# A decoder trunk on one core: two gate tiles moved from the attention to the front of the seven-product units, and the branches' elementwise work drawn together

## The chip, the cores and the metric

The kernel runs as one program on one core of a Trainium2 chip. Its time is the device time of one execution in microseconds; of several runs the median is taken. The engines are PE (TensorE, matrix products), DVE (VectorE, elementwise), ACT (ScalarE, activations and copies), POOL (GpSimd) and SP (SyncE, which here only starts transfers). Each engine works through its own queue in order and meets the others through semaphores.

## The reference, cut to what matters

Two layers over a sequence of 1024 tokens with 1024 channels, in float32. Each layer:

```python
h = rmsnorm(x, norm_mix_g[l])
q, k, v, f_logit, cx, cb, cc, px, gate_logit = split(h @ w_in[l])
a = forgetting_attention(rmsnorm(q), rmsnorm(k), v, log_sigmoid(f_logit + forget_b[l]))  # 8 heads of 64
y_attn = a @ w_attn_out[l]
y_conv = (cb * conv3(cc * cx)) @ w_conv_out[l]                # depthwise, 256 channels
y_pool = pooling_mixer(px, pool_w[l], pool_scale[l])          # trailing means over 2, 4, 8, 16 positions
g = sigmoid(gate_logit)                                       # three gates of 1024 channels
x = x + (g[0] * y_attn + g[1] * y_conv + g[2] * y_pool) @ w_o[l]
h = rmsnorm(x, norm_ffn_g[l])
x = x + (silu(h @ w_gate) * (h @ w_up)) @ w_ffn_out[l]
```

## The kernel before, in words

Everything is kept transposed: 128 channels on the partitions, the tokens in two halves of 512 along the free axis. Every float32 operand is split into a high and a low part that TensorE multiplies at full rate, and each product is three matmuls: high by high, high by low, low by high (mm3, lines 219 to 221). The split of a weight tile is one cast on ACT (L115) and one subtraction on DVE (L116); of an activation tile, a cast (L224) and a subtraction (L225). Raw weights (tag "wr") have two slots, the high and low parts (tags "wh" and "wl") three; the weight pieces of the seven-product units use the same three.

A layer goes through these stages:

1. v and the forget logits (v_run; v_evac writes v to DRAM through staging tiles whose four tags vtags turn).
2. Eleven seven-product units (sevens, m_unit). Each makes a block of 256 output channels by 1024 tokens with seven products in place of eight. The products are over sums and differences of parts of h, the forms: b11, b21 and b22 are parts of h, t1 to t4 are made by make_form on DVE and ACT, four tiles each, every tile with a high and a low part. prepare makes the units' weight pieces, four to a unit. The eleven units compute q, k, the conv and pool branches' inputs (which go to DRAM) and six gate tiles (SGATES).
3. The attention, four pairs of heads, eight query blocks and two heads a pair. scores, turn and values are issued one chain apart, and between them fill issues steps of gate tiles. A gate tile (gate_unit) is a projection of 128 gate channels: for each half of the tokens 24 matmuls, in four steps, then a Tanh from PSUM on ACT (L667) and a store to DRAM (gate_away, on SP). GATES says how many of them there are: two before the first pair and three in each pair.
4. The last four gate tiles. Between their steps the branches' elementwise work is issued: for each half c of the branch channels the loads cc_in and fetch, then cx_evac, cb_evac and px_evac, nearly all on DVE.
5. The merge (merge_unit): output projections of the three branches, gated and added. The gate tiles are fetched from DRAM by get_t; those in the set plain were stored as raw logits and get their Tanh there (L1082).
6. The output projection, norms and the feed-forward part.

The helper `plan` is a queue of units; `step` runs the next step of the current unit, and `prefetch` loads weights for the units ahead as long as no more than two tiles are pending. The framework places the instructions of each engine in a queue of its own making, by the order of the program and by what its timing model takes to be ready; the order within a stage can therefore differ from that of the text.

The tiles of stage 2 that matter here come from one ring of five buffers, which the forms t1 and t3 and the copies of the products share:

```python
def mring(name, dt=F32):
    return mp.tile([P, HN], dt, tag="ring", name=name, bufs=MRING)   # MRING = 5
```

In make_form the four tiles of t1 stay in the ring (diffs); t2 is made from them in place, and t4 from t2. In a unit the first product is copied out of its bank into the ring (copy("p1"), L837), and the fourth product is then accumulated on the same bank.

Of the kernel before, what the change touches and what calls it, by code (L numbers as in the profile page):

```python
# [9 lines left out]
F32 = mybir.dt.float32  # L10
F32R = mybir.dt.float32r
# [5 lines left out]
P = 128  # L17
S = 1024
D = 1024
KT = D // P  # L20
NH = 2
HN = S // NH
# [6 lines left out]
OFF_CX, OFF_CB, OFF_CC, OFF_PX, OFF_G = 1544, 1800, 2056, 2312, 2568  # L29
# [12 lines left out]
FINE = 4  # L42
# [1 line left out]
TURNS_LAST = {3: ((1, 2),), 4: ((3, 2),), 6: ((5, 2),), 7: ((6, 1), (7, 1))}  # L44
QDEF = 2
SGATES = 6
GATES = (2, 3, 3, 3, 3)


class Unit:  # L50
# [9 lines left out]
def trunk_kernel(ctx: ExitStack, tc: tile.TileContext, x, norm_mix_g, w_in, forget_b, q_norm_g, k_norm_g,  # L60
# [37 lines left out]
    plan = deque()  # L98
# [49 lines left out]
    def prefetch():  # L148

        pending = sum(len(u.specs) for u in plan if u in loaded_w)  # L150
        for u in plan:
            if u in loaded_w:
                continue
            if pending and pending + len(u.specs) > LOOK:
                break
            loaded_w[u] = [load_f(s) if s[1] == "f" else load(s) for s in u.specs]
            pending += len(u.specs)
# [36 lines left out]
    def drain():  # L194
        while step():
            pass
        while later:
            run_later(True)

    def wspec(src, rows, c0, cols):  # L200

        return (src[rows[0]:rows[1], c0:c0 + cols].rearrange("(k p) m -> p k m", p=P), ((rows[1] - rows[0]) // P, cols))
# [342 lines left out]
    for l in range(L):  # L545
# [7 lines left out]
        def mring(name, dt=F32):  # L553
            return mp.tile([P, HN], dt, tag="ring", name=name, bufs=MRING)
        win = w_in[l]
# [26 lines left out]

        v_dram = [dr.tile([P, 2, KT, P], F32R, tag=f"vd{p}", name="vd") for p in range(PAIRS)]

        vtags = deque(("q2", "q3", "qkh", "qkl"))

        def v_evac(p0, n, banks):

            for q in range(2):
                for j in range(0, 4, 2):  # L590
                    tag = vtags[0]
                    vtags.rotate(-1)
                    dst = mp.tile([P, HN], F32R, tag=tag, name="vst").rearrange("p (e j c) -> p e j c", e=2, j=2)
                    for jj in range(2):
                        src = banks[j + jj][:, q * P:(q + 1) * P].rearrange("p (e c) -> p e c", e=2)
                        A.copy(out=dst[:, :, jj, 0:HD], in_=src)
                        V.tensor_tensor(out=dst[:, :, jj, HD:P], in0=src, in1=dst[:, :, jj, 0:HD].bitcast(F32),
                                        op=ALU.subtract)
                    G.dma_start(out=v_dram[p0 + q][:, :, 4 * n + j:4 * n + j + 2, :], in_=dst)
# [58 lines left out]
        def gate_away(br, m, n, t):  # L658
            td = dr.tile([P, HN], F32, tag=f"td{br}{m}{n}", name="td")
            nc.sync.dma_start(out=td, in_=t)  # L660
            spilled.add((br, m, n))
            tgate[br, m, n] = td
# [133 lines left out]
        def make_form(name):  # L796

            add_h = lambda k, n, part: h[k, n][part].bitcast(F32)
            for k in range(KH):
                if name in ("t1", "t3"):  # L800
                    x, y = ((k, 1), (k, 0)) if name == "t1" else ((KH + k, 1), (k, 1))
                    t = mring("form")
                    lows = mp.tile([P, HN], F32, tag="q1", name="lows")
                    V.tensor_tensor(out=t, in0=add_h(*x, 0), in1=add_h(*y, 0), op=ALU.subtract)
                    V.tensor_tensor(out=lows, in0=add_h(*x, 1), in1=add_h(*y, 1), op=ALU.subtract)
                    V.tensor_tensor(out=t, in0=t, in1=lows, op=ALU.add)
                else:
                    x = (KH + k, 1) if name == "t2" else (KH + k, 0)
                    t = diffs[k]
                    V.tensor_tensor(out=t, in0=add_h(*x, 0), in1=t, op=ALU.subtract)  # L810
                    V.tensor_tensor(out=t, in0=t, in1=add_h(*x, 1), op=ALU.add)
                if name == "t1":
                    diffs[k] = t
                hi = mp.tile([P, HN], F32R, tag=f"{name}h{k}", name=name)
                lo = mp.tile([P, HN], F32R, tag=f"{name}l{k}", name=name)
                hilo(hi, lo, t)
                mforms[name].append((hi, lo))

        def m_unit(u):
            kind, at = pairs[u]  # L820
            t = {}

            def finish(e, n, src):
                if kind == "g":
                    br, m = divmod(at + e, KT)
                    gate_away(br, m, n, src)
                    plain.add((br, m, n))
                elif kind in ("cc", "cx", "cb", "px"):
                    branch[kind, e, n] = dr.tile([P, HN], F32, tag=f"{kind}{e}{n}", name="brd")
                    nc.sync.dma_start(out=branch[kind, e, n], in_=src)  # L830
                else:
                    norm_qk(at + e, kind, n, src)

            def copy(name):
                def ev(bank):
                    t[name] = mring(name)
                    return A.copy(out=t[name], in_=bank)  # L837
                return ev

            def add(name, e, n):  # L840
                def ev(bank):
                    done = V.tensor_tensor(out=t[name], in0=bank, in1=t[name], op=ALU.add)
                    finish(e, n, t[name])
                    return done
                return ev

            def c21(bank):
                t["c21"] = mring("c21")
                A.copy(out=t["c21"], in_=bank)
                finish(1, 0, t["c21"])  # L850

            def u2(bank):
                done = copy("u2")(bank)
                if u == 0:
                    make_form("t4")
                return done

            seven(u, mforms, {"p1": copy("p1"), "c11": add("p1", 0, 0), "p5": copy("p5"), "u2": u2,
                              "c12": add("u2", 0, 1), "c22": add("p5", 1, 1), "c21": c21})

        next_first.run = v_run(0)
# [2 lines left out]
        for _ in range(FINE * NH):  # L864
            step()
        plan.append(Unit([wspec(win, (r, r + D // 2), OFF_V + 2 * P, 2 * P) for r in (0, D // 2)], v_run(2)))
        prefetch()
        prepare(0)
        make_form("t1")
        for _ in range(FINE):  # L870
            step()
        make_form("t2")
        drain()
        prepare(1)
        make_form("t3")
        for _ in range(SGATES):
            gates.popleft()
        for u in range(len(work)):
# [252 lines left out]
        for c in range(2):  # L1131
            cc_in(c)
            for n in range(NH):
                cx_evac(c)(n, fetch("cx", c, n))
                for _ in range(FINE):
                    step()
            for n in range(NH):
                cb_evac(c)(n, fetch("cb", c, n))
                px_evac(c)(n, branch["px", c, n])
                for _ in range(FINE):  # L1140
                    step()
        for mm in range(4):
            plan.append(merge_unit(mm))
        prefetch()
# [290 lines left out]
        u = n_in  # L1435
# [73 lines left out]
```

## Time and profile before

| what | value |
|---|---|
| median of 3 runs | 2873.04 us (2869.07 to 2873.19) |
| the profiled execution | 2866.68 us |
| its span, first to last instruction | 2864.9 us |
| mean granted clock of TensorE | 0.992 of full speed |

The profile is of one execution. Times within it count from the first instruction. Layer 0 takes about the first half of the span: v to about 78 us, the units to about 310, the attention to about 580, the last gates to about 621, then the merge. Layer 1 has the same stages some 1422 us later.

### The profile page before, as it was taken

The page shows a single profiled execution, that of the slowest core. Times are in us where ns is not written, and L with a number is a line of the kernel's source. Part 1 is how long each engine was busy: PE and PEld are TensorE (multiplying, and loading weights), DVE is VectorE, ACT ScalarE, POOL GpSimd, SP SyncE. Part 2 cuts the span into 40 slices and gives each one's busy share as a digit, 9 for nine tenths or more (in the row PEclk, how much of TensorE's full clock was granted, in tenths as well). Part 3 has the DMA queues.
Part 4 walks back from the last instruction along what each step waited for, and adds up shares of the span by engine and source line. Part 5 has one row for each costly group of instructions (what it writes and reads, how often), then busy time and mean ns, then how long its engine had stood idle before and what let it go on. Part 6 is the DMA issues. An engine that isn't in the chain of part 4 may idle for free.

```text
span 2864.9 us, 38079 instructions
## 1 busy us (share of the span) xinstructions
PE 2807.6 (98%) x13224; PEld 2322.3 (81%) x13224; DVE 2080.1 (73%) x3869; ACT 1313.2 (46%) x2137; POOL 584.7 (20%) x1100
## 2 busy tenths in 40 slices
PE   8899999999999999999998999999999999999999
PEld 8788888878888888878796888888788888888887
DVE  8886298878575676758788763988785867766675
ACT  5665266533453444432356643655334444444222
POOL 2110333000411111334010104330003111223430
PEclk9999999999999999999999999999999999999999
DMA  7343856267533444699353438552765244557992
GB/s 226 114 129 111 213 140 159 78 221 226 187 104 118 133 143 152 204 289 310 111 150 105 140 100 224 140 157 84 249 214 181 95 133 147 162 162 232 309 284 93
DMA packets 378089, 481.90 MB, mean 168 GB/s; under 512 B 35336, under 2 KB 227336, under 8 KB 376872
## 3 DMA queue, kind: packets, MB, share of 16 engines
q1 hardware_dynamic: 261864, 260.19, 29.4%
q0 software_dynamic: 116032, 219.27, 25.9%
q8 instruction: 104, 1.70, 0.2%
q14 instruction: 89, 0.73, 0.1%
HBM read 319.91 MB, written 159.45 MB: 167 GB/s over the span
## 4 chain that ended last, share of the span: by engine, by line
PE 84%; DVE 6%; DMA 5%; issue 3%; ACT 1%; POOL 0%; SPq 0%; DVEq 0%; ACTq 0%; POOLq 0%
PE dps L219 25%; PE dps L221 25%; PE dps L220 25%; PE pt L738 2%; PE pv L755 2%; DMA td<-tg 1%; PE qk L713 1%; PE qk L714 1%; DMA px<-brd 1%; DVE wl L116 1%; PE dps L615 1%; PE dps L617 1%; PE dps L616 1%; DMA acd<-al 1%; DMA wr<-in_w_in_dram 1%
## 5 line engine op out<-in xcount | busy, mean ns | idle before, releaser
L219 PE MATMUL dps<-t,wsh 128*128 128x512 f32 x992 | 388.5, 392 | 17.5 <-ACT p L837 17.5
L220 PE MATMUL dps<-t,wsh 128*128 128x512 f32 x992 | 387.6, 391 | 0.0
L221 PE MATMUL dps<-t,wsl 128*128 128x512 f32 x992 | 387.4, 391 | 0.0
L221 PE MATMUL dps<-hh,wsl 128*128 128x512 f32 x744 | 289.8, 390 | 0.0
L219 PE MATMUL dps<-hh,wsh 128*128 128x512 f32 x744 | 289.7, 389 | 0.0
L220 PE MATMUL dps<-hl,wsh 128*128 128x512 f32 x744 | 289.6, 389 | 0.0
L378 ACT CAST wsh<-ws 128x1024 fp32r<-128x1024 f32 (+2 forms) x172 | 167.3, 973 | 253.6 <-DVE ws L370 176.7
L219 PE MATMUL dps<-hh,wh 128*128 128x512 f32 x704 | 278.7, 396 | 0.0
L220 PE MATMUL dps<-hl,wh 128*128 128x512 f32 x704 | 278.0, 395 | 0.0
L221 PE MATMUL dps<-hh,wl 128*128 128x512 f32 x704 | 277.1, 394 | 0.0
L379 DVE TENSOR_TENSOR wsl<-wr,wsh 128x512 fp32r<-128x512 f32 (+4 forms) x172 | 151.1, 878 | 158.0 <-ACT wsh L378 157.8
L379 DVE TENSOR_TENSOR wsl<-ws,wsh 128x1024 fp32r<-128x1024 f32 (+2 forms) x172 | 193.0, 1123 | 87.7 <-ACT wsh L378 87.7
L219 PEld LDWEIGHTS dps<-t,wsh 128*128 128x128 f32 x992 | 187.1, 189 | 57.8 <-ACT p L837 18.4
L115 ACT CAST wh<-wr 128x1024 fp32r<-128x1024 f32 (+1 forms) x116 | 118.4, 1021 | 231.6 <-PE dps L220 171.6
L116 DVE TENSOR_TENSOR wl<-wr,wh 128x1024 fp32r<-128x1024 f32 (+1 forms) x116 | 138.1, 1191 | 112.8 <-ACT wh L115 112.6
L221 PEld LDWEIGHTS dps<-t,wsl 128*128 128x128 f32 x992 | 187.2, 189 | 39.2
L220 PEld LDWEIGHTS dps<-t,wsh 128*128 128x128 f32 x992 | 187.2, 189 | 38.5
L378 ACT CAST wsh<-wr 128x512 fp32r<-128x512 f32 (+4 forms) x172 | 133.6, 777 | 134.5 <-PE dps L220 132.2
L1196 POOL DMA_DIRECT2D acd<-ah x122 | 64.9, 532 | 547.0 <-ACT ah L224 544.2
L221 PE MATMUL dps<-ach,wsl 128*128 128x512 f32 x448 | 174.6, 390 | 0.0
L219 PE MATMUL dps<-ach,wsh 128*128 128x512 f32 x448 | 174.4, 389 | 0.0
L220 PE MATMUL dps<-acl,wsh 128*128 128x512 f32 x448 | 174.4, 389 | 0.0
(271 smaller groups left out, 6550.7 us busy)
## 6 DMA issues: line engine op xcount, KB each, us to landing
wr<-in_w_ffn_in_dram SPq DMA_DIRECT2D x40, 1024.0 KB, 5.5
acl<-acd POOLq DMA_DIRECT2D x136, 256.0 KB, 6.8
ach<-acd POOLq DMA_DIRECT2D x136, 256.0 KB, 6.6
acd<-ah POOLq DMA_DIRECT2D x122, 256.0 KB, 2.3
acd<-al POOLq DMA_DIRECT2D x122, 256.0 KB, 2.5
tin<-td SPq DMA_DIRECT2D x96, 256.0 KB, 3.7
wr<-in_w_in_dram SPq DMA_DIRECT2D x44, 512.0 KB, 4.1
wr<-in_w_in_dram SPq DMA_DIRECT2D x22, 1024.0 KB, 5.3
```

The costliest lines, as they stand in the source:

```text
L115: A.copy(out=hi[:, 0:cnt], in_=rv)
L116: V.tensor_tensor(out=lo[:, 0:cnt], in0=rv, in1=hi[:, 0:cnt].bitcast(F32), op=ALU.subtract)
L219: T.matmul(dst, lhsT=wh, rhs=rh, start=start and k == 0, stop=False, skip_group_check=again)
L220: T.matmul(dst, lhsT=wh, rhs=rl, start=False, stop=False, skip_group_check=again)
L221: T.matmul(dst, lhsT=wl, rhs=rh, start=False, stop=stop and k == n - 1, skip_group_check=again)
L378: A.copy(out=hv, in_=src)
L379: V.tensor_tensor(out=lv, in0=src, in1=hv.bitcast(F32), op=ALU.subtract)
L615: T.matmul(dst, lhsT=hh[:, cols], rhs=wh[:, k % 4, :], start=first, stop=False)
L616: T.matmul(dst, lhsT=hh[:, cols], rhs=wl[:, k % 4, :], start=False, stop=False)
L738: T.transpose(pt[:, j * P:(j + 1) * P], lg[:, c0 + j * P:c0 + (j + 1) * P], idf)
L755: T.matmul(pv[:, e], lhsT=vs[:, j, :], rhs=pps[c][:, j - c0 // P], start=j == 0, stop=j == i)
L1196: G.dma_start(out=d[:, i, :], in_=t)
```

## The change

Two gate tiles per layer leave the attention (the second and the fourth pair have two instead of three). They are taken from the far end of the gate list and computed between v and the first unit, evacuated by a plain copy and stored as raw logits, so that get_t applies their Tanh at the merge. The forms t3 and t4 and the first two calls of prepare are issued among the steps of these two tiles; t4 was issued in the first unit before. The tiles of t3 leave the ring for the tag q3, which the staging of v gives up. In the last gates, all of a half's elementwise work is issued before eight steps of the gates, where four steps stood between its parts; so sixteen of the 32 steps come after it.

```diff
-GATES = (2, 3, 3, 3, 3)
+COVER = 2
+GATES = (2, 3, 2, 3, 2)
...
-        vtags = deque(("q2", "q3", "qkh", "qkl"))
+        vtags = deque(("q2", "qkh", "qkl"))
+
+        def staging(name, dt=F32):
+            vtags.rotate(-1)
+            return mp.tile([P, HN], dt, tag=vtags[0], name=name)
...
-                    t = mring("form")
+                    t = mring("form") if name == "t1" else mp.tile([P, HN], F32, tag="q3", name="form")
...
-            def u2(bank):
-                done = copy("u2")(bank)
-                if u == 0:
-                    make_form("t4")
-                return done
-
-            seven(u, mforms, {"p1": copy("p1"), "c11": add("p1", 0, 0), "p5": copy("p5"), "u2": u2,
+            seven(u, mforms, {"p1": copy("p1"), "c11": add("p1", 0, 0), "p5": copy("p5"), "u2": copy("u2"),
...
+        def plain_evac(br, m):
+            def evac(n, b):
+                t = staging("tg")
+                A.copy(out=t, in_=b)
+                gate_away(br, m, n, t)
+                plain.add((br, m, n))
+            return evac
+
+        covers = [gates.pop() for _ in range(COVER)]
+        plan.extend(proj_unit(wspec(win, (0, D), OFF_G + br * D + m * P, P), plain_evac(br, m)) for br, m in covers)
         prefetch()
-        prepare(0)
         make_form("t1")
         for _ in range(FINE):
             step()
         make_form("t2")
+        for _ in range(FINE + 1):
+            step()
+        prepare(0)
+        make_form("t3")
+        for _ in range(FINE * NH - 1):
+            step()
+        prepare(1)
+        make_form("t4")
         drain()
-        prepare(1)
-        make_form("t3")
...
             for n in range(NH):
                 cx_evac(c)(n, fetch("cx", c, n))
-                for _ in range(FINE):
-                    step()
             for n in range(NH):
                 cb_evac(c)(n, fetch("cb", c, n))
                 px_evac(c)(n, branch["px", c, n])
-                for _ in range(FINE):
-                    step()
+            for _ in range(FINE * NH):
+                step()
```

## Rows read from the trace of the kernel before

**Rows 1.** The page's busy time in us (share of the span) and instructions.
```profile
PE 2807.6 (98%) x13224; PEld 2322.3 (81%) x13224; DVE 2080.1 (73%) x3869; ACT 1313.2 (46%) x2137; POOL 584.7 (20%) x1100
```

**Rows 2.** Whom PE waited for: us in total, times, longest us.
```profile
PE dps L219 <- ACT p L837: 17.5, 2, 9.3
PE dps L221 <- DVE wl L116: 7.2, 3, 3.0
PE dps L219 <- ACT wch L115: 4.8, 2, 3.4
```

**Rows 3.** Windows at the first unit and merge: length, busy time by engine, clock, DMA.
```profile
core 0: us, PE busy (x) PEld busy (x) DVE busy (x) ACT busy (x) POOL busy (x), PEclk, DMA share, GB/s
86.20:100.20 14.00, 4.69 (x12) 3.02 (x11) 14.00 (x24) 7.10 (x11) 0.00 (x0) 0.63 0.24 75
1508.80:1522.80 14.00, 5.77 (x14) 3.85 (x13) 14.00 (x25) 6.14 (x9) 0.00 (x0) 0.65 0.24 75
620.90:645.00 24.10, 17.39 (x61) 13.05 (x60) 19.92 (x28) 7.29 (x12) 0.00 (x0) 0.86 0.52 171
2043.20:2065.00 21.80, 16.57 (x57) 11.99 (x56) 18.65 (x26) 6.84 (x10) 0.00 (x0) 0.84 0.54 181
```

**Rows 4.** Timeline of PE in layer 0's first unit: start, length, idle before.
```profile
95.89 0.80 PE L219 MATMUL dps<-t,wsh 128*128 128x512 f32 x1 [9.31 <-ACT p L837]
96.48 0.63 PE L220 MATMUL dps<-t,wsh 128*128 128x512 f32 x1
96.91 0.63 PE L221 MATMUL dps<-t,wsl 128*128 128x512 f32 x1
...
104.03 0.39 PE L219 MATMUL dps<-t,wsh 128*128 128x512 f32 x1
...
106.75 0.39 PE L219 MATMUL dps<-hh,wsh 128*128 128x512 f32 x1
```

**Rows 5.** Timeline of DVE and of ACT there.
```profile
93.94 1.29 DVE L225 TENSOR_TENSOR t<-form,t 128x512 fp32r<-128x512 f32 x2
...
104.77 0.68 DVE L225 TENSOR_TENSOR t<-form,t 128x512 fp32r<-128x512 f32 x1
...
95.26 0.58 ACT L837 COPY p<-dps 128x512 f32<-128x512 f32 x1 [1.19 <-DVE t L225]
```

**Rows 6.** Windows of layer 0's attention: whole, densest, pairs two, four, start.
```profile
347.90:579.50 231.60, 228.27 (x1287) 189.65 (x1286) 199.40 (x687) 139.44 (x295) 56.52 (x128) 1.00 0.49 128
368.00:448.00 80.00, 79.46 (x465) 66.22 (x464) 76.27 (x265) 51.53 (x109) 24.69 (x56) 1.00 0.57 144
402.20:456.80 54.60, 54.03 (x320) 45.38 (x318) 51.06 (x176) 35.62 (x76) 18.74 (x43) 1.00 0.70 170
514.50:573.00 58.50, 57.70 (x324) 48.42 (x323) 48.99 (x171) 34.02 (x72) 5.86 (x15) 1.00 0.23 73
...
348.00:368.00 20.00, 19.94 (x98) 15.80 (x98) 12.95 (x61) 9.44 (x26) 6.52 (x17) 1.00 0.59 169
```

**Rows 7.** DVE's groups in layer 0's attention: busy us, mean ns, idle before.
```profile
L116 DVE TENSOR_TENSOR wl<-wr,wh 128x1024 fp32r<-128x1024 f32 x11 | 13.4, 1220 | 1.6 <-ACT wh L115 1.6
```

**Rows 8.** Timeline of DVE in layer 0's last gates.
```profile
589.80 1.23 DVE L116 TENSOR_TENSOR wl<-wr,wh 128x1024 fp32r<-128x1024 f32 x1 [3.23 <-ACT wh L115]
...
595.12 0.70 DVE L1011 TENSOR_TENSOR z<-cin,cc 128x512 f32<-128x512 f32 x1 [2.18 <-DMA cin<-brd]
...
600.06 0.69 DVE L1021 TENSOR_TENSOR cv<-cin,cv 128x512 f32<-128x512 f32 x1 [3.18 <-DMA cin<-brd]
...
604.43 1.23 DVE L1045 TENSOR_TENSOR sa<-px 128x1024 f32<-128x1024 f32 x1 [1.58 <-DMA px<-brd]
...
632.41 1.29 DVE L1072 TENSOR_TENSOR pd<-sb,pd 64x512 fp32r<-64x512 f32 x2
```

**Rows 9.** Timeline of SP's queue at layer 0's merge: weight loads.
```profile
624.33 0.38 SPq L110 DMA_DIRECT2D wr<-in_w_attn_out_dram  x1
626.60 0.38 SPq L110 DMA_DIRECT2D wr<-in_w_conv_out_dram  x1
```

More of the change, by code (lines that the diff above doesn't have):

```diff
@@ L590, in v_evac @@
                 for j in range(0, 4, 2):
-                    tag = vtags[0]
-                    vtags.rotate(-1)
-                    dst = mp.tile([P, HN], F32R, tag=tag, name="vst").rearrange("p (e j c) -> p e j c", e=2, j=2)
+                    dst = staging("vst", F32R).rearrange("p (e j c) -> p e j c", e=2, j=2)
                     for jj in range(2):
```

## The prediction

> **What bounds the kernel now.** I read the page's busy shares first: PE is busy for 98% of the span, DVE for 73% [rows 1]. A busy share counts a waiting TensorE only roughly, so the second view is who PE waited for: the two longest waits are one of 9.3 and one of 8.2 us on a copy of the first product (L837), and several of about 3 us on weight splits, L116 and L115 [rows 2]. The third view prices these places. At full speed twelve matmuls of 512 columns start from 104.03 to 106.75, that is 0.2267 us each [rows 4]. In the 14 us after the first unit's third product only 12 matmuls are seen in layer 0 and 14 in layer 1 [rows 3], worth 2.72 and 3.17 us: 11.3 and 10.8 us are lost there, 22.1 in all. Around the start of the merge 61 matmuls take 24.1 us and 57 take 21.8 us [rows 3], worth 13.8 and 12.9: 10.3 and 8.9 us are lost, 19.2 in all. These four places hold 41 us. The attention, 231.6 us per layer, has no wait of such a length, but there DVE is nearly full as well: 76.27 of 80 us in its second part and 51.06 of 54.6 us in the second pair [rows 6].
>
> The reader should see why the first wait is so long. The copy of product one sits on ACT at 95.26, right behind the last subtraction of form t3 on DVE, 93.94 and two of them [rows 5]. The ring has five slots; the four t1 tiles are held until t4 is made from them, every t3 tile passes through the fifth, and the copy, which asks for a slot after them, gets it when t3 is done. The product that accumulates into that bank waits for the copy. After the stall the clock is at the lower of its two levels, 1.2 instead of 2.4 GHz: matmuls 0.43 us apart instead of 0.2267 [rows 4], and a mean granted clock of 0.63 over the window [rows 3].
>
> **Part one, the cover.** It moves two gates (96 matmuls, 96 x 0.2267 = 21.8 us of PE) per layer ahead of the first unit, moves prepare, t3 and t4 ahead of it, and takes t3 off the ring. Is 21.8 us enough? In the kernel before t4's last subtraction ends at 104.77 + 0.68 = 105.45 [rows 5]. The wait of 9.31 us ended at 95.89 [rows 4], so the three products before it (36 matmuls, 8.2 us) began near 78.4; now they begin 21.8 us later, near 100. DVE does two weight splits of 1.22 us more [rows 7], so even if all of the unit's own work still ran in between, t4 is done by 107.9. What PE needs first is ring space, which t3 no longer takes, then t1 and t2 (made long before), t3 at its sixth product (5 x 12 x 0.2267 = 13.6 us after the start, 113.6) and t4 after the next unit's first (119). The margin is 6 us for t3 and 11 for t4. So the stall and the slow clock behind it go, except for the norms' own small waits; I keep 0.8 us per layer for those: 22.1 - 1.6 = 20.5 us gained. Bounds: 0, if ring or slots stall it as before, and 22.1.
>
> What moves with the gates: two loads of 512 KB on SP, two casts and two splits, four evacuations (ACT copies now, no Tanh) and four stores on SP. SP has little else there, and the splits are in the sum above. The weight pieces of the unit share three slots with the gates: its first piece waits for v's end, the second for the first gate's end, the third for the second's, and that one is needed four products (10.9 us) later for a cast and a split, about 2 x 1.22 us. I cost that at nothing; without the margin it is a wait of those 2.4 us. Staging with three tags instead of four makes each fourth v tile wait for the first one's store; the banks that PE asks for next are read by the third, so nothing, at most 3 us per layer if DVE is held up behind it. The t3 tiles take turns in one buffer, four turns of five operations of some 0.68 us [rows 5], 13.6 us, inside the 21.8. At the merge four more Tanh per layer run on ACT, busy there for 7.29 of 24.1 us [rows 3]; uncovered they are about 4 x 0.68 = 2.7 us per layer.
>
> **Part two, the attention with two gates fewer.** PE loses 21.8 us of work per layer, DVE two splits: 199.40 - 2.44 = 196.96 us [rows 6, 7]. If the attention shortened by all of the 21.8 us it would last 209.8. DVE's own floor: its first 20 us hold only 12.95 us of work [rows 6]; the other 184.0 us at 76.27/80 = 95.3%, its share in the densest 80 us, take 193.0; in all 213.1. So 3.3 us per layer don't come back, and I take 5, since the thinned pairs leave PE no spare matmuls at the end: 10 us lost over both layers. Bounds: 0 (DVE at 98%), and from the windows of the two thinned pairs at the 93.5% which the second pair shows (51.06/54.6): (51.06 - 1.22)/0.935 = 53.3 of 54.6 and (48.99 - 1.22)/0.935 = 51.1 of 58.5, so 1.3 and 7.4 us shorter for 10.9 removed each, 13.1 per layer, 26 in all.
>
> The Trainium skill, on its page Perfetto Trace Analysis (Identifying the Most-Contended Engine), holds that occupancy tells how near Vector is to its limit but not how near the tensor engine is. By PE's 54.03 us of 54.6 the second pair would shorten by the whole gate and nothing would be lost; by the page's rule it can shorten at most to DVE's 49.8, and 6.1 us of that gate stay, which over both layers makes 12.2 where I take 10. The rule speaks against this part, and the sum above already leans its way.
>
> **Part three, the branches' elementwise work.** Nothing is added or removed; the loads and the DVE work of each half come ahead of eight steps instead of between four and four. Before, DVE idles 3.23 us behind a split that waits for its slot, then 2.18, 3.18 and 1.58 us for loads [rows 8], which on SP stood behind stores that wait for their gate. That is 10.2 us, and the chain ends at 632.41 + 1.29 [rows 8]. Its lateness makes both merge waits: the split L116, and then w_conv_out, whose load is only issued at 626.60 when a raw slot comes free [rows 9]. If the chain ended 10 us earlier both waits, 3.0 and 3.4 us [rows 2], would go, and with them the slow clock. But the three weight loads still pass through two raw slots one after another, and splits rank behind the elementwise work. I take 6 us per layer, 12 of 19.2. Bounds: 0 and 18.
>
> **Sum.** 20.5 + 12 - 10 = 22.5 us, or 0.8%. The profiled execution took 2866.68 us around a span of 2864.9; the median of the three runs is 2873.04. The gain is counted in the profile and taken off the median: 2850.5.
>
> **Rivals.** (1) The merge wait stays, because SP's order was set by memory coming free and not by the stores: 20.5 - 10 = 10.5, 2862.5. For it speaks the slot chain [rows 9], against it the three waits for loads in a row [rows 8]. (2) The thinned pairs stay near the 93.5% window: 20.5 + 12 - 26 = 6.5, 2866.5. (3) Slower: DVE alone sets the attention's pace and it doesn't shorten at all, so the 43.5 us of moved matmuls all come on top: 20.5 + 12 - 43.5 = -11, 2884. It decides once more than 8.1 of each gate's 10.9 us are lost (32.5/4); the second pair is near that (9.6), the fourth, with DVE at 48.99 of 58.5, is not [rows 6]. (4) The attention loses nothing and the merge is nearly clean: 20.5 + 18 = 38.5, 2834.5. (5) The cover does not cover: DVE or the slots come half as late again, 10 instead of 20.5: 2861. (6) The thinned pairs open gaps long enough for the clock to fall. It stood at 1.00 in every attention window [rows 6], and after the 9.31 us wait matmuls started 0.43 us apart [rows 4]. One fall per thinned pair, with eight slow matmuls as after the merge waits (8 x 0.2 = 1.6 us) and a gap of 3 us, costs 18 us: 22.5 - 18 = 4.5, 2868.5.
>
> The Trainium skill's page TensorE: Matmul & The Clock Gate (What's actually happening) says that the throttled state is the default and activity releases it; the trace agrees at the stall, with 0.43 against 0.2267 us, and rival 6 is what it would do here.
>
> **How the numbers follow.** The forecast gets 0.47, its own range 2840 to 2860. Rival 1 gets 0.17, 2 gets 0.12, 3 gets 0.07, 4 gets 0.09, 5 gets 0.04, 6 gets 0.04. The range, 2835 to 2868, takes in rivals 1, 2, 5 and the edges of 4 and 6, and leaves out some 0.15. A difference of 0.2% is 5.7 us, about what these runs can tell from none: below 2867.3 lie the forecast, rivals 1, 4 and 5 and half of 2, 0.83; rival 3 is slower, 0.07; the rest is the same, 0.10.
>
> **What would show it.** Right: no wait on L837 at the first unit and a granted clock of 1.00 there; t4 made before the unit starts; a DVE share of 93 to 97% in the attention, which is some 17 us shorter; elementwise idle under 4 us, its end some 10 us nearer to the start of the last gates, the merge's two waits under 2 us each. Wrong: PE waits on qk, pt or pp that add up to over 13 us per layer in the attention, a wait on a gate's split in the last gates because it ranks behind the elementwise work, or the same L116 and L115 waits at the merge.

## The result and the profile after

The changed kernel takes 2826.3 us (median of four runs, 2823.8 to 2827.7) where the kernel before takes 2871.1 beside it: a ratio of 0.9848, 95% interval 0.9827 to 0.9869. The forecast was 2850.5 with a range of 2835 to 2868. The sign was right, the gain is about twice the forecast one, and the time lies below the range. The profiled execution took 2827.06 us around a span of 2825.3; its span is 39.6 us shorter than that of before, while the medians are 44.8 us apart, because the profiled execution of before lay 4.4 us under its median and this one 0.8 us over its own.

A table of stages shows where these come from. Each stage runs from the start of one matmul in TensorE's timeline to the start of another: v's first, the first unit's first, the first score, the last value product, the first product with the attention's output, and the first with the merge's result. Layer 0 stands first, then layer 1, in us.

| stage | before | after | change, both layers |
|---|---|---|---|
| v and cover | 60.1, 55.9 | 81.6, 78.0 | +43.6 (96 matmuls more in each) |
| seven-product units | 253.6, 254.4 | 241.5, 241.5 | -25.0 |
| attention | 247.7, 246.6 | 227.2, 225.9 | -41.3 (88 matmuls fewer in each) |
| last gates | 41.2, 41.2 | 39.4, 39.4 | -3.6 (8 fewer) |
| merge | 83.2, 81.9 | 74.3, 73.7 | -17.1 (as many) |
| all else | | | +3.8 |

The page's busy row of TensorE, and then whom it waited for (us in total, times, longest us):

```profile
PE 2795.7 (99%) x13224; PEld 2312.8 (82%) x13224; DVE 2073.9 (73%) x3869; ACT 1315.2 (47%) x2145; POOL 581.5 (21%) x1100
```

```profile
PE qk L716 <- DVE mx L723: 2.5, 2, 2.0
...
PE dps L222 <- DVE wcl L117: 1.5, 2, 0.8
```

The wait on the copy of a first product, 17.5 us in [rows 2], is gone, and so are the waits of 3 us at the merge; of weight splits only wcl's, 1.5 us in two waits, is still waited for there for more than 0.2 us. Windows of the same lengths answer to [rows 3], from the start of the first unit and of the merge. (Those of [rows 3] start behind the unit's third product; at that place, from 108.2 us on, it is 62 matmuls in 14 us at 1.00.)

```profile
100.20:114.20 14.00, 14.00 (x63) 11.47 (x62) 9.87 (x15) 9.79 (x14) 0.00 (x0) 1.00 0.29 95
1502.90:1516.90 14.00, 14.00 (x63) 11.50 (x62) 8.66 (x13) 9.79 (x14) 0.00 (x0) 1.00 0.29 95
608.20:632.30 24.10, 23.03 (x100) 18.29 (x99) 21.58 (x34) 10.11 (x16) 0.00 (x0) 1.00 0.71 227
2009.60:2031.40 21.80, 21.14 (x93) 17.14 (x92) 19.23 (x31) 9.02 (x14) 0.00 (x0) 1.00 0.69 221
```

63 matmuls run in 14 us where 12 and 14 ran, 100 and 93 at the merge where 61 and 57 ran, and the granted clock is 1.00 in all four, where it was 0.63 to 0.86. TensorE's timeline at the unit's start, then VectorE's last subtraction of t4 and ScalarE's copy of product one:

```profile
100.23 0.39 PE L220 MATMUL dps<-hh,wsh 128*128 128x512 f32 x1
...
102.73 0.39 PE L222 MATMUL dps<-hh,wsl 128*128 128x512 f32 x1
```

```profile
102.79 0.68 DVE L226 TENSOR_TENSOR t<-form,t 128x512 fp32r<-128x512 f32 x1
```

```profile
103.86 0.58 ACT L840 COPY p<-dps 128x512 f32<-128x512 f32 x1
```

TensorE enters at 100.2 as forecast (near 100), and the copy runs 0.7 us after its product's end (102.73 + 0.39). t4 ends at 103.5, inside the bound of 107.9, though not before the unit starts, as the forecast's last part said it would; it is needed only at the next unit. Windows of layer 0's attention, which answer to [rows 6]: whole, 80 dense us, pairs two, three and four, and the start:

```profile
358.60:568.90 210.30, 207.33 (x1192) 170.97 (x1191) 192.97 (x685) 133.82 (x289) 53.95 (x129) 1.00 0.51 135
...
378.00:458.00 80.00, 79.52 (x464) 66.01 (x464) 76.26 (x266) 52.73 (x112) 25.28 (x57) 1.00 0.54 145
...
411.00:466.40 55.40, 53.54 (x316) 44.63 (x314) 50.67 (x176) 35.77 (x76) 18.63 (x42) 1.00 0.67 166
466.40:512.10 45.70, 45.03 (x253) 36.87 (x254) 43.79 (x163) 29.69 (x65) 11.53 (x30) 1.00 0.51 139
512.10:568.90 56.80, 56.63 (x335) 47.11 (x334) 53.09 (x182) 37.01 (x80) 5.31 (x15) 1.00 0.25 79
...
358.60:378.60 20.00, 19.94 (x103) 15.79 (x101) 14.39 (x68) 10.30 (x28) 6.99 (x19) 1.00 0.77 195
```

The last two pairs before, up to the last value product, were:

```profile
456.80:514.50 57.70, 56.21 (x312) 46.78 (x311) 48.42 (x168) 34.72 (x73) 13.26 (x29) 1.00 0.51 133
514.50:579.50 65.00, 64.07 (x361) 53.55 (x360) 54.47 (x179) 37.88 (x78) 5.86 (x15) 1.00 0.23 75
```

Three things are to be seen. The whole window is 210.3 us long, 0.5 us from the 209.8 that the forecast gave for "shortened by all of it". Pair two, which lost a gate on paper, isn't shorter than before (55.4 us against 54.6), while pair three, which lost none, is 45.7 us long and was 57.7: a gate's matmuls don't stay in the pair for which they are written. And VectorE's busy time fell from 199.40 to 192.97 us, by 6.4 and not by the two splits' 2.4.

### The profile page after: what moved, and what is told of

Read it like the earlier page. It is cut to its first block, busy times and chain, and to the rows that moved or that the text cites. A ratio compares the mean times of both kernels' runs of the same rounds, so it can differ in the third digit from the quotient of the medians.

```text
span 2825.3 us, 38083 instructions
## 1 busy us (share of the span) xinstructions
PE 2795.7 (99%) x13224; PEld 2312.8 (82%) x13224; DVE 2073.9 (73%) x3869; ACT 1315.2 (47%) x2145; POOL 581.5 (21%) x1100
```

## The experiments

Each run's time is a median beside runs of the kernel before, whose medians were 2867.3 to 2867.5 us. The changed kernel's 2826.3 stood beside 2871.1, so a difference between it and one of these runs can be off by up to some 4 us.

**Elementwise order alone.** The kernel before with the change's last hunk only.

```diff
                 cx_evac(c)(n, fetch("cx", c, n))
-                for _ in range(FINE):
-                    step()
...
                 px_evac(c)(n, branch["px", c, n])
-                for _ in range(FINE):
-                    step()
+            for _ in range(FINE * NH):
+                step()
```

> The kernel before with the new order of the branches' elementwise work alone. If the merge's 17.1 us in the two layers (8.9 and 8.2 us between the stage lengths of before and after) come from that order, the time falls to about 2871 - 17 = 2854 us, and the merge stage is some 74 us long instead of 83. The forecast's term for it was 12 us: 2859. Rival: the order gives its gain only together with the earlier end of the attention in the changed kernel, and alone it gives under 6 us: 2865 to 2871.

2851.6 us, ratio 0.9948 (0.9933 to 0.9963): 15.7 us faster. The merge stage is 74.9 and 76.1 us long. The order does it alone, so the rival falls.

**All but the elementwise order.** The same hunk taken out of the changed kernel.

```diff
-            for _ in range(FINE * NH):
-                step()
+                for _ in range(FINE):
+                    step()
```

> The changed kernel with the old order of the elementwise work. If the parts add up, it loses the merge's 17 us and nothing else: 2826 + 17 = 2843 us, the attention still some 21 us shorter than before. Rival: cover and thinner attention have shifted the branches' loads so that the old order is now good enough as well: within 5 us of 2826.

2840.3 us, ratio 0.9911 (0.9896 to 0.9926): 14.0 us of the gain are lost, the merge stage is 83.2 and 84.3 us long, and the attention keeps its 226.6 and 224.9. The parts add up, a little under the 17 expected; against the run with the loads first (the next one) the loss is 16.3 us. SyncE's queue of this run in layer 0 shows the cause; the second fence is VectorE there, the third SyncE's queue of the changed kernel.

```profile
567.16 0.42 SPq L1007 DMA_DIRECT2D cin<-brd  x1
577.05 0.32 SPq L663 DMA_DIRECT2D td<-tg  x1
577.54 0.33 SPq L1007 DMA_DIRECT2D cin<-brd  x1
577.96 0.48 SPq L663 DMA_DIRECT2D td<-tg  x1
```

```profile
586.74 0.69 DVE L1023 TENSOR_TENSOR z<-cin,cc 128x512 f32<-128x512 f32 x1 [7.18 <-DMA cin<-brd]
...
590.67 0.69 DVE L1033 TENSOR_TENSOR cv<-cin,cv 128x512 f32<-128x512 f32 x1 [2.18 <-DMA cin<-brd]
```

```profile
567.54 1.38 SPq L1007 DMA_DIRECT2D cin<-brd  x3
572.52 0.32 SPq L1048 DMA_DIRECT2D px<-brd  x1
572.89 0.43 SPq L1007 DMA_DIRECT2D cin<-brd  x1
573.36 0.44 SPq L1048 DMA_DIRECT2D px<-brd  x1
577.47 0.93 SPq L663 DMA_DIRECT2D td<-tg  x2
```

In the old order the second load comes 10 us after the first, right behind a store of a gate (td) that waits for its gate, and VectorE idles 7.18 and 2.18 us for such loads. In the new order all loads of the half are issued before the first store.

**Loads first, alternation kept.** The changed kernel with the old alternation, but the loads of a half issued ahead of it (px_load is px_evac's own load, taken out of it).

```diff
+            cx_at = [fetch("cx", c, n) for n in range(NH)]
+            cb_at = [fetch("cb", c, n) for n in range(NH)]
+            px_load(c)
             for n in range(NH):
-                cx_evac(c)(n, fetch("cx", c, n))
+                cx_evac(c)(n, cx_at[n])
+                for _ in range(FINE):
+                    step()
...
-            for _ in range(FINE * NH):
-                step()
```

> The changed kernel with the old alternation of the elementwise work and the last gates' steps, but with all the loads of a half (cx, cb, px) issued ahead of its first step. If the old order was slow because its loads stood on SyncE behind gate stores, as the forecast said, most of the 14 us between the run without the new order (2840) and the changed kernel (2826) are gained: 2826 to 2830. Rival: the alternation itself holds the work back, because each quarter of it is placed behind the steps written before it: 2836 to 2842.

2824.0 us, ratio 0.9845 (0.9829 to 0.9862): the whole gain, with a merge stage of 73.5 and 74.2 us. The place of the loads in the queue is the cause; the place of VectorE's work among the steps is not.

**Thinner attention alone.** The kernel before, the two gates moved to its last gates.

```diff
-GATES = (2, 3, 3, 3, 3)
+GATES = (2, 3, 2, 3, 2)
```

> The kernel before with two gates fewer in the attention (its fourth number of gates 2 for 3, its last 2 for 3), done in the last gates instead, six there for four; forms, ring and elementwise order as before. Theory: TensorE alone sets the pace in the attention, so it gets shorter by the whole 21.8 us per layer (stage of 247.7 to about 226), and the last gates longer by as much. The total is then that of before, 2871, or up to 17 us less where the longer last gates hide the merge's waits: 2854 to 2871. Rival, the forecast's term: VectorE's floor keeps 5 us per layer, the attention stage is about 231 to 232 us long, and the total is 10 us more than by the theory.

2863.2 us, ratio 0.9987 (0.9978 to 0.9997). The attention is 227.1 and 225.6 us long, as in the changed kernel: with 88 matmuls (19.9 us at 0.2267) fewer it is 20.6 and 21.0 us shorter. Nothing is lost, and the forecast's term falls. The merge stage stays slow (81.5 and 82.4 us), although the last gates are 20 us longer: with the loads in their old order, more cover did not help.

**Ten gates in the attention.** The changed kernel with two more gates per layer taken out and done in the last gates.

```diff
-GATES = (2, 3, 2, 3, 2)
+GATES = (2, 2, 2, 2, 2)
```

> The changed kernel with ten gates in the attention and six last gates; the cover stays at two. In the run with four gates in the cover the attention did not get shorter than in the changed kernel, and 74 matmuls of the last gates were issued in it, so that the last gates lasted 22.6 us and TensorE then waited 18 us for w_conv_out's cast. Theory: the attention is at VectorE's floor (20 us of start plus 176 us of work at the 95.3% of its densest 80 us, about 205 us where the changed kernel has 210.3), so it stays within 5 us of 226; but the longer last gates hide the elementwise work again and the merge's wait is gone: 2832 to 2844. Rival: the wait comes from VectorE's backlog out of the thinner attention, whatever the last gates hold: the wait stays and the total is 2860 or more.

2854.5 us, ratio 0.9952 (0.9937 to 0.9967): 28.2 us slower than the changed kernel, between the figures of the two theories. The attention is 225.0 and 223.4 us long, within the 5 us of 226, as expected; but it took in only 24 matmuls of the last gates, so that 72 matmuls (16.3 us) fewer per layer brought 2.2 and 2.4 us. 14.1 + 13.9 = 28.0 us are lost there, the whole difference. No wait for w_conv_out is left (merge stage 73.2 us in both layers), so the rival falls; the theory's total is missed by 10. The windows from 17 us after the first score, as in [rows 6], then two of TensorE's waits:

```profile
359.30:567.30 208.00, 195.45 (x1119) 158.21 (x1118) 190.98 (x683) 130.74 (x283) 54.79 (x129) 1.00 0.48 126
...
1774.20:1980.60 206.40, 195.42 (x1119) 158.10 (x1117) 190.94 (x683) 130.56 (x283) 55.05 (x128) 1.00 0.47 127
```

```profile
PE pt L741 <- DVE pp L745: 7.3, 8, 1.8
PE qk L716 <- DVE mx L723: 7.2, 17, 1.4
```

Here a floor on VectorE's side is seen: 208.0 and 206.4 us, with TensorE waiting for VectorE's pp and mx (for VectorE 11.5 us in all in layer 0's attention, where the changed kernel waits 2.3). The changed kernel, at 210.3 and 208.9, is 2.3 and 2.5 us longer, and its two further splits are 2.4 us of VectorE's work: by this count it stands about on that floor, though its TensorE hardly waits yet.

**Eleven gates.**

```diff
-GATES = (2, 3, 2, 3, 2)
+GATES = (2, 3, 2, 2, 2)
```

> The changed kernel with eleven gates in the attention (2 at its start, then 3, 2, 2, 2) and five last gates. TensorE's work in the attention then is 226.5 - 10.9 = 215.6 us per layer. Theory: VectorE's floor is near 223 us (17 us before the window, 20 us of start, 177 us of work at 95.3%), so the attention gets at most 3.5 us shorter and TensorE fills it with matmuls of the last gates; the total is 2824 to 2834. Rival: there is no floor yet, the attention shortens by the whole gate to about 216 us and the total is 2826.

2842.2 us, ratio 0.9909 (0.9894 to 0.9924). The attention doesn't shorten (227.4 and 225.2 us), but TensorE's work there hasn't shrunk either: 46 matmuls of the last gates fill the place of the 48 removed, placed there when the framework made the queues. Layer 0's attention:

```profile
341.30:568.70 227.40, 224.39 (x1266) 185.01 (x1265) 194.38 (x686) 135.57 (x291) 65.88 (x151) 1.00 0.54 142
```

So this run says nothing of a floor; it decides neither for the theory nor for the rival, and the total missed my range by 8 us. The loss comes later: from the last value product on, 121.8 us pass for 496 matmuls, where the changed kernel takes 113.6 for 494. The number is the same, the order is not: the merge's first product comes after 132 of these matmuls instead of 174, a gate's products stand behind it, and TensorE waits there for weight splits:

```profile
600.87 0.50 PE L220 MATMUL dps<-art,wh 128*128 128x512 f32 x1 [2.18 <-ACT wh L116]
...
605.48 0.80 PE L222 MATMUL dps<-hh,wl 128*128 128x512 f32 x1 [3.42 <-DVE wl L117]
```

The first waits for its weights' load: ScalarE's cast at 599.77 follows 2.69 us of idle time that end with the landing of w_attn_out, issued at 592.62. The second starts on VectorE at 604.21, right behind other work. Whether there is more to it wasn't followed further.

**Four gates in the cover, ten in the attention.**

```diff
-COVER = 2
-GATES = (2, 3, 2, 3, 2)
+COVER = 4
+GATES = (2, 2, 2, 2, 2)
```

> The changed kernel with four gates in the cover and ten in the attention (two at its start and for each of the four pairs), last gates as in the changed kernel. Theory: TensorE sets the attention's pace until VectorE is full; VectorE's 193.0 us less two splits of 1.22 stay under the 205 us that the attention's TensorE work then takes, so the attention shortens by another 20.5 us per layer and the total stays within 6 us of 2826. Rival: a pair cannot be shorter than its VectorE work; the second pair, 55.4 us with 50.7 of VectorE, would shorten by 10.9 to 44.5 us, under that work, and keeps 5 us or more per layer: 2836 to 2846.

2877.6 us, ratio 1.0031 (1.0020 to 1.0043): slower even than the kernel before, and both theories missed. The attention is 229.8 and 224.8 us long, no shorter, filled with 74 matmuls of the last gates. The last gates then take 22.6 us for 39.4. The windows of layer 0's last gates and of the merge's start, and TensorE's wait:

```profile
594.00:616.50 22.50, 22.50 (x102) 18.67 (x101) 16.98 (x31) 8.85 (x14) 4.80 (x9) 1.00 0.97 334
616.50:640.00 23.50, 8.34 (x37) 6.57 (x35) 17.92 (x30) 5.66 (x9) 0.00 (x0) 0.77 0.57 202
```

```profile
PE dps L220 <- ACT wch L116: 36.1, 2, 18.3
```

The elementwise work now has 22.5 us of cover, and TensorE stands 18 us at w_conv_out's cast. With as many gates in the attention and six last gates, two runs up, that wait is not there.

**No gate in the pairs.**

```diff
-GATES = (2, 3, 2, 3, 2)
+GATES = (2, 0, 0, 0, 0)
```

> The changed kernel with no gate in the four pairs (two at the attention's start as before; the ten others move to the last gates, fourteen there). It shows what the attention takes when TensorE has no other work, that is VectorE's floor or the chain's. VectorE then has 193.0 - 10 x 1.22 = 180.8 us to do. If it runs without gaps, the attention's stage is some 181 to 185 us long (98 to 100% busy); at the 95.3% that the forecast used, 190 to 197 us; if the chain through TensorE, ScalarE and VectorE sets the pace, longer still and VectorE under 93% busy. The ten gates cost 109 us per layer in the last gates, so the total is 2826 + 2 x (stage + 109 - 226.5): 2953 at 181 us, 2985 at 197.

3013.0 us. The attention's stage in the two layers, then TensorE's longest wait:

```profile
342.20:557.90 215.70, 160.81 (x812) 116.86 (x811) 184.35 (x677) 119.06 (x264) 67.12 (x149) 0.88 0.40 103
1830.80:2049.70 218.90, 164.26 (x812) 122.10 (x811) 184.81 (x677) 119.11 (x264) 68.13 (x150) 0.85 0.39 103
```

```profile
PE qk L716 <- DVE mx L723: 36.3, 60, 9.3
```

The windows that answer to [rows 6], which leave out the start, and one of 80 us:

```profile
359.20:557.90 198.70, 153.06 (x779) 111.21 (x780) 181.57 (x665) 116.70 (x258) 55.55 (x124) 0.88 0.33 88
1847.90:2049.70 201.80, 157.47 (x783) 117.13 (x784) 183.02 (x672) 117.57 (x262) 56.56 (x126) 0.85 0.33 88
400.00:480.00 80.00, 59.23 (x294) 42.87 (x293) 72.06 (x272) 46.45 (x107) 33.78 (x74) 0.85 0.55 135
```

The stages are 215.7 and 218.9 us long, the third of the cases named: the granted clock is 0.88 and 0.85, and TensorE waits for mx 60 times. VectorE is busy for 85% of the stage. But past the start it is busy for 91%, about as much as with ten and twelve gates (92%), and the window is 9.3 us shorter in layer 0 than with ten gates, for 9.4 us less of VectorE's busy time, and 4.6 us shorter in layer 1 for 7.9. So VectorE's work and the chain through the engines, partly at the low clock, bound together; the run doesn't separate them. They bound already: 455 matmuls fewer than in the changed kernel, worth 103 us, make the attention only 11.4 and 7.0 us shorter.

**t3 off the ring, nothing else.** The kernel before with one tag changed.

```diff
-        vtags = deque(("q2", "q3", "qkh", "qkl"))
+        vtags = deque(("q2", "qkh", "qkl"))
...
-                    t = mring("form")
+                    t = mring("form") if name == "t1" else mp.tile([P, HN], F32, tag="q3", name="form")
```

> The kernel before with t3 taken off the ring (its own buffer, v's staging with three tags), nothing else. Theory: the copy's wait for a ring slot was only where VectorE's backlog of t3 and t4 showed; without it the copy runs at once, but TensorE comes to a stand a few products later, at the pieces and at t3 and t4, which VectorE finishes no earlier. The gain is under 8 us in all, 2863 to 2871, and a wait of several us shows at a weight piece or at t3. Rival: the slot itself was the cause, and most of the 22 us at the first units go: 2849 to 2853.

2863.3 us, ratio 0.9987 (0.9977 to 0.9996): 4 us, as the theory said. ScalarE's timeline in layer 0, then VectorE's, then TensorE's:

```profile
81.65 0.59 ACT L837 COPY p<-dps 128x512 f32<-128x512 f32 x1 [1.63 <-PE dps L221]
...
94.06 1.17 ACT L224 CAST t<-form 128x512 fp32r<-128x512 f32 x2 [3.05 <-DVE form L811]
97.09 0.59 ACT L837 COPY p<-dps 128x512 f32<-128x512 f32 x1 [1.87 <-DVE t L225]
```

```profile
95.68 1.29 DVE L225 TENSOR_TENSOR t<-form,t 128x512 fp32r<-128x512 f32 x2
```

```profile
97.73 0.80 PE L219 MATMUL dps<-hh,wsh 128*128 128x512 f32 x1 [7.84 <-ACT p L837]
```

The first copy runs at 81.65 instead of 95.26 [rows 5]: the ring did hold it. But the next copy, of product three, waits in its turn, and TensorE stops one product later, for 7.84 us instead of 9.31. The casts ahead of it on ScalarE end at 95.2; the wait of 1.87 us is the copy's own and ends with a split of a form on VectorE, at 96.97. Four tiles of t1 and the first copy fill the five slots, so most likely it waits for the slot that t4's first tile leaves; the trace doesn't name the slot, and a longer ring wasn't run. The theory had the wait at a weight piece or at t3, and there it isn't.

**Cover, t3 on the ring.** The changed kernel with one line as before.

```diff
-                    t = mring("form") if name == "t1" else mp.tile([P, HN], F32, tag="q3", name="form")
+                    t = mring("form")
```

> The changed kernel with t3 back on the ring (v's staging and the covers' copies keep their three tags). Theory: the cover alone does the work, since t3 and t4 are made before the first unit asks for ring space, whichever buffer they pass through: no change, 2821 to 2831 us, no wait over 2 us at the first units. Rival: the ring's fifth slot is still asked for in turn, t3 holds back t4 and the copy of product one, and up to 9 us per layer come back: up to 2844.

2824.3 us, ratio 0.9854 (0.9839 to 0.9868), units 241.5 us in both layers. With a cover, it makes no difference that t3 passes through the ring.

**Cover, forms written where they were.**

```diff
-        for _ in range(FINE + 1):
-            step()
         prepare(0)
-        make_form("t3")
-        for _ in range(FINE * NH - 1):
-            step()
-        prepare(1)
-        make_form("t4")
         drain()
+        prepare(1)
+        make_form("t3")
```

(and t4 again behind product four)

> The changed kernel with the forms written where they were before: t3 only after the covers' last step, t4 after the first unit's fourth product; cover, t3's own buffer, thinner attention and elementwise order stay. Theory: the 21.8 us of cover are what VectorE needs, but it must also be given the work in time; with t3 and t4 issued behind the covers, the copies of products one and three still stand on ScalarE behind the forms' casts, and 4 to 8 us per layer of the 12.5 gained at the first units go: 2834 to 2842. Rival: VectorE and ScalarE have room under the cover and the forms are started there anyway: 2821 to 2831.

2825.2 us, ratio 0.9850 (0.9835 to 0.9864), units 241.5 us in both layers. My theory fell: the forms' place in the program doesn't matter either; they are made under the cover anyway, t4's last subtraction starting at 104.87 us in layer 0 instead of 102.79. (t3 on the ring and the forms at their old place, both at once, wasn't run.)

**One gate of cover.**

```diff
-COVER = 2
-GATES = (2, 3, 2, 3, 2)
+COVER = 1
+GATES = (2, 3, 3, 3, 2)
```

> The changed kernel with one gate in the cover and thirteen in the attention (2 at its start and 3, 3, 3, 2 in the pairs). TensorE enters the first unit 10.9 us earlier, near 89, while VectorE finishes t3 and t4 near 103 and 107. By the forecast's need times t3 is wanted at 89 + 13.6 = 102.7 and t4 at 108: the stall is nearly gone with one gate, 0 to 3 us per layer come back, 2826 to 2832. Rival: the copies of products wait on ScalarE behind the casts of t3 and t4, as in the run with the ring change alone, and about half of the gain at the first units goes: 2836 to 2840.

2834.0 us, ratio 0.9887 (0.9872 to 0.9901). The units take 244.8 and 243.9 us, so 3.3 and 2.4 us come back, about as expected, in a wait for a weight piece and not for t3:

```profile
103.09 0.50 PE L220 MATMUL dps<-hh,wsh 128*128 128x512 f32 x1 [2.40 <-ACT wsh L379]
```

One gate already gives 19.3 of the 25.0 us at the units (253.6 - 244.8 and 254.4 - 243.9). The total missed the expected 2832 by 2.

No version tried is measurably faster than the changed kernel; three (2824.0, 2824.3, 2825.2) can't be told from it.

## Why the prediction was wrong

By its terms, forecast and measured: part one 20.5 and 25.0; part two -10 and +1.3 (41.3 + 3.6 out of the attention and last gates, 43.6 into v); part three 12 and 17.1; all else 0 and -3.8. The sums are 22.5 and 39.6. Of the 17.1 us between them part two makes 11.3, part three 5.1 and part one 4.5, and the rest takes 3.8 away. The mechanisms of parts one and three were right in the main; the loss of part two did not occur, and this is the step that made the prediction fail.

**Part two, the step that failed: "in all 213.1. So 3.3 us per layer don't come back, and I take 5".** TensorE still sets the attention's pace. With 88 matmuls (19.9 us) taken out, the stage is 20.6 and 20.7 us shorter, and 20.6 and 21.0 us in the run with the thinner attention alone; the window lasts 210.3 us, less than the 213.1 that was held to be VectorE's least. A floor exists, but it is lower: 208.0 and 206.4 us with ten gates, where the forecast's own rule would give 210.5. Two numbers in it were off. It took VectorE's busy time as a fixed amount of work, 196.96 us. The rows say otherwise: added up over VectorE in the attention's window, the single instructions last 239.2 us before, more than the window's 231.6, because many are still running when the next has begun. In the changed kernel's timeline:

```profile
430.71 0.68 DVE L723 CUSTOM_DVE_ANT_0 lg<-qk,negcb 128x512 f32<-128x512 f32 x1
431.32 0.08 DVE L723 DVE_READ_ACCUMULATOR2_ANT mx<- 128x1 f32 x1
431.32 0.69 DVE L745 TENSOR_TENSOR pp<-pt,pp 128x512 fp32r<-128x512 f32 x1
```

0.68 us of work hold the engine for 0.61. With less idle time between them more of them overlap: the sum fell by 3.5 us (to 235.7) and the busy time by 6.4. And the first 20 us took 14.39 us of work instead of 12.95, so less was left for the rest. With these two numbers the same rule gives 20 + (192.97 - 14.39)/0.953 = 207.4 us, under TensorE's 209.8, and no loss. That is worked out after the fact, and the rule stays rough: for ten gates it gives 20 + (190.98 - 14.42)/0.953 = 205.3, where 208.0 was measured. The extra 1.7 us "since the thinned pairs leave PE no spare matmuls" had no row behind it.

The Trainium skill's page Perfetto Trace Analysis (Optimizing Scalar/DVE Operations) says that the fixed data-access overhead of a Scalar or DVE operation looks about twice as long in the profile as it keeps the engine busy, since its write-acknowledgement half overlaps with the next instruction. The rows above agree in kind, with 0.61 us between starts for a length of 0.68. The rule of its section Identifying the Most-Contended Engine, which the forecast weighed, gave 12.2 us of loss by pair two; the pair did stay at 55.4 us, yet none was lost, since pair three ran the shorter for it, 45.7 us for 57.7.

Rival 2 fell on the same ground: pairs are not units of work. Rival 3 fell, but its mechanism is one step away: with ten gates, 72 matmuls fewer in the attention bring 2.2 and 2.4 us. Rival 4, which had the attention lose nothing and the merge nearly clean (2834.5), was the right one in mechanism. That its 38.5 us come within about a microsecond of the 39.6 between the spans is partly luck: it kept part one at 20.5, 4.5 too low, and 3.8 us were lost elsewhere.

**Part one** was right in its mechanism and 4.5 us short. Both windows of 14 us [rows 3] saw 22.1 us of the loss, but the units held 1052 matmuls (238.5 us) in 253.6 and 254.4 us: 15.1 and 15.9 too many, of which 3.0 are left in each. The stall with its slow clock was 12.1 and 12.9 us, more than the 11.3 and 10.8 that the windows saw. The 0.8 us per layer kept for the norms' waits stood against nothing: in the units of the changed kernel TensorE has no wait over 0.1 us, and the one of note before (1.0 us, in layer 1) lies at 1551 us, behind the windows. The reading of the first wait was off in one point: the copy at 95.26 didn't get its slot "when t3 is done". The fourth tile of t3 is only begun then, on VectorE before the change:

```profile
95.14 0.68 DVE L804 TENSOR_TENSOR form<-hh,hh 128x512 f32<-128x512 f32 x1
```

The two splits at 93.94 [rows 5] that the copy follows are those of t3's third tile and t4's first. So taking t3 off the ring couldn't free it of VectorE, as that run shows; the cover didn't depend on this point. Of the listed parts only the cover mattered; the ring or the forms' place, each by itself, could stay as it was. Rival 5 fell.

**Part three** was right that loads stood behind stores, which the run with the loads first shows, and took 12 between bounds of 0 and 18 because the weight loads "still pass through two raw slots". They do, yet their splits come early enough: the merge's waits for them are 1.5 us in all for wcl and 0.2 for wqh's cast. VectorE's timeline in layer 0's last gates, after:

```profile
577.24 0.07 DVE L1052 MEMSET sa<- 128x16 f32 x1 [4.64 <-DMA ad<-at]
...
588.50 0.69 DVE L226 TENSOR_TENSOR cul<-cv,cuh 128x512 fp32r<-128x512 f32 x1 [0.99 <-ACT cuh L225]
...
613.38 1.29 DVE L1084 TENSOR_TENSOR pd<-sb,pd 64x512 fp32r<-64x512 f32 x2
```

Of the 10.2 us of idle time [rows 8], 1.2 are left (0.99, and 0.21 later), under the 4 named as the sign. A wait for the store of the attention's output, ahead of them, isn't in the forecast's count; it grew from 3.2 to 4.64 us, so with it the idle time fell by 7.6 us, from 13.4 to 5.8. The chain ends 45.8 us after the last value product where it ended 54.2 after it: 8.4 us nearer, 10 forecast. Rival 1 fell.

**The clock** (rival 6) stayed at 1.00 in every window shown of the changed kernel. It does fall when the attention is thinned to the end: 0.88 and 0.85 with no gate in the pairs. The Trainium skill's page TensorE: Matmul & The Clock Gate (What's actually happening) has the throttled state as the default; these two rows are in keeping with that, but can't show which state is the default. VectorE's share in the attention is 91.8% (192.97 of 210.3), under the 93 to 97% named as the sign; but that range didn't follow from the forecast's own figures, which give the same 91.8% (196.96 us of a window "some 17 us shorter" than 231.6).

The +3.8 us outside the stages of the table (start, output projections, feed-forward parts) were not traced further, but no edit touches these parts, and they differ as much among the runs: from the merge's result of layer 0 to v of layer 1 the fourteen kernels take 738.0 to 742.3 us (741.0 before, 742.3 after), from layer 1's to the end 740.1 to 745.1 (740.1 and 742.0).

Of the 24.2 us between the forecast 2850.5 and the median 2826.3, 17.1 are those of the sum. The forecast started from 2873.0 where the kernel before had 2871.1 beside the changed one, which makes 2.0, and the medians lie 5.1 us further apart than the spans.

## What to carry to other kernels

A busy time read from a window with gaps isn't the work that must fit into a shorter one: instructions that overlap make it shrink. Before you cost a thinner stage by an engine's busy share, measure that engine's floor by taking out too much: two gates fewer were free here, and the next two cost 28 us.

Where one queue carries both stores that wait for results and loads that others need, put the loads first; that alone was worth 14 to 16 us, and 20 us more of cover could not replace it. When a copy waits for a slot, ask what the next one will wait for: freeing the first copy's slot moved the stall by one product and won 4 us, while work for TensorE ahead of it won 25.

## What the runs showed of the hardware that had not been expected

VectorE's 128x512 operations of 0.68 us start 0.60 to 0.61 us apart when they follow each other, so that before the change the instruction lengths add up to more than the window (239.2 us in 231.6). And TensorE's granted clock fell to 0.88 and 0.85 in the mean over the attentions with no gate in the pairs, and to 0.85 over 80 us of them (400 to 480) in which the longest single wait is 1.8 us and the waits are many; before, the low level stood behind single waits of 3 to 9 us [rows 2, 4].
